# Two diffusion-transformer blocks on one core: value projections laid out channel-major, and the planner's view of a PSUM tile

## The chip, the cores and the metric

One core of a Trainium2 chip runs the whole program: two layers of a block with four kinds of token mixers and an MLP, on 512 image tokens and 256 context tokens. The metric is the device time of one execution in microseconds; three runs of the kernel before took 1811.11, 1812.51 and 1814.94 us.

The engines are TensorE (PE in the views; PEld is its weight load), VectorE (DVE), ScalarE (ACT), GpSimd (POOL) and SyncE (SP), whose queue issues all the transfers of this kernel.

## The reference

Each of the two layers does the following (widths: model 1024, MLP 4096, heads of 64):

```
mod, mod_c = (silu(c), silu(c_ctx)) @ mod_w[l] + mod_b[l]      # six vectors of 1024 each, for image and context
u  = modulate(rmsnorm(h,  norm1), sh1, sc1)  @ w_in            # 512 tokens
uc = modulate(rmsnorm(hc, norm1), csh1, csc1) @ w_in           # 256 context tokens
y_a = ssd_mixer(...)      # conv, silu, two directions of a chunked state scan, gated norm
y_b = diff_mixer(...)     # differential attention: softmax(q1 k1) - lam * softmax(q2 k2), times values
y_c = gqa_mixer(...)      # normed q and k, 4 query heads on 2 key heads
y_d = mla_mixer(...)      # low-rank q and kv, each normed and multiplied by a second weight
h  = h + g1 * (concat(y_a, y_b, y_c, y_d) @ w_out)
h  = h + g2 * (relu(modulate(rmsnorm(h, norm2), sh2, sc2) @ w1) ** 2 @ w2)
```

In the attentions the image queries look at the 256 context and 512 image tokens. The context goes through the same (its queries see the context alone) in layer 0 only. The result is rmsnorm(h) after layer 1.

The columns of w_in that matter here are those of the differential attention (q, k and values, 256 columns each: two groups of 128, dq0, dq1, dk0, dk1, dv0, dv1) and the 128 value columns of the grouped attention.

## The kernel before

**Layout and arithmetic.** Activations lie channel-major: 128 channels in the partitions, 768 tokens (512 image, called XS, then 256 context, called CS) in the columns. A product of full accuracy is three fp32r matmuls: each operand is split into a high and a low part (`split`: ScalarE copies the high part, VectorE or GpSimd subtracts it for the low part), and high x high, high x low and low x high are summed in PSUM. `gemm` does that over the eight tiles of 128 input channels. `big_gemm` sums into a PSUM tile of 1024 columns (tag S, two of them), `side_gemm` into tiles of 512 (tag g, four of them), first the image tokens, then the context. The result of such a projection is channel-major.

**Values.** The product of the attention weights with the values wants the tokens of the values in the partitions. Before, the 384 value columns (differential 256, grouped 128) are therefore computed token-major: `v_start` takes six PSUM regions, one for each 128 tokens, and `v_step` adds one channel tile k to each of them, with the normed activations as the stationary operand and 384 weight columns as the moving one. `v_weights` loads these weights from an array of their own, wv. At the end ScalarE copies 256 columns of each region (dv) and VectorE 128 (gv).

**The start.** x, the modulation weights of layer 0 (four blocks of 2 MB, `mod_dma`) and the first weights are loaded. The norm's statistics are summed (`n_ms`), the modulation is summed block by block (`mod_load`, PSUM tile pm; `mod_done`, PSUM tile pn), and after each block two norm tiles are made (`xn_start`: n_t on VectorE, the high part xn_h on ScalarE, the low part xn_l on VectorE). Between the blocks the values take each norm tile as it comes (`v_step`, PSUM tiles pv, pva, pvb).

**The mixers.** `mixers` runs several tracks as generators: support (all the other projections in the order dk0, dq0, dk1, dq1 and then ORD0, at last `mla_prep`), the attentions one after another (differential j = 0, 1, grouped, MLA), the scan (`ssd_track`), the modulation still to be summed, and the output projection. `Weave` interleaves them by a virtual clock: each step yields a cost, multiplied by its track's weight (TUNE), and the track with the earliest clock goes next. An attention waits until a flag is set: `ready(j)` once the q and k tiles of group j are stacked. Stacking (`stack`) is 16 transfers for each of dk0, dq0, dk1 and dq1. In layer 1 the order is dq0, values, dk0, dq1, dk1, then ORD1, and the weights of the values are split on VectorE.

**The planner.** All instructions go to `Plan.take` first, which notes each one's cost by a formula and what it depends on: two accesses of one tile depend on each other if they overlap and one of them writes. `Plan.order` then plays the program through with these costs. Of an engine's instructions that are ready, the one of the lowest rank goes first (rank is the place in the program; an evacuation of PSUM is put 200 places ahead). Transfers are played at 250 KB per us, one after another, and 1.2 us later for landing. GpSimd's work lengthens VectorE's by 30% of the overlap. Buffers of a tag are given out in the order in which they are first asked for. The order that comes out is each engine's instruction order on the chip; the semaphores follow from the real dependencies.

Weights are staged in float32 in 7 tiles of 128x512 (tag wr) and split into 4 tiles of 2x512 (tag ws).

Of the kernel before, what the change touches and what calls it, by code (L numbers as in the profile page):

```python
# [19 lines left out]
P = 128  # L20
D = 1024
# [16 lines left out]
def _r(c, n=P):  # L38
# [10 lines left out]
    "ckv": _r(C_CKV),  # L49
}  # L50
T_COLS = np.concatenate([_r(C_DV, 256), _r(C_GV)])
# [67 lines left out]
class Later:  # L119


    def __init__(self, pool, shape, dt, name, tag, bufs):
        self.args = (pool, shape, dt, name, tag, bufs)
        self.dt, self.tag, self.bufs = dt, tag, bufs
        self.made = None
# [6 lines left out]
    def ap(self):  # L132
        pool, shape, dt, name, tag, bufs = self.args
        if self.made is None and bufs == 1:
            self.made = pool.tile(list(shape), dt, name=name, tag=tag, bufs=1)
        elif self.made is None:
            self.made = pool.tile(list(shape), dt, name=name, tag=f"{tag}_{self.slot}", bufs=1)
        return self.made
# [12 lines left out]
class Pool:  # L151
    def __init__(self, pool):
        self.pool = pool

    def tile(self, shape, dt, name, tag, bufs):
        t = Later(self.pool, shape, dt, name, tag, bufs)
        return View(t, (), t.base)
# [11 lines left out]
class Plan:  # L169
# [5 lines left out]
    GROUP = 1.0  # L175

    def __init__(self, tc):
        self.tc, self.nc = tc, tc.nc
        self.ops = []
# [5 lines left out]
    def cost(self, eng, name, args, kw, out):  # L185
# [3 lines left out]
        if eng == "PE":  # L189
# [5 lines left out]
            m = w.width()  # L195
# [19 lines left out]
        return 0.45, 1.2  # L215

    def take(self, eng, fn, name, args, kw):
        out = kw["out"] if "out" in kw else args[0]
        writes = [x for x in (out, kw.get("accum_out")) if isinstance(x, View)]
# [3 lines left out]
        if not (eng == "PE" and op is not None and op.eng == "PE" and op.out is out.t and op.cost + cost <= self.GROUP):  # L223
            op = Op(len(self.ops), eng)
            op.out = out.t if isinstance(out, View) else None
            op.bytes = self.bytes if eng == "SP" else 0
# [3 lines left out]
        op.late = late  # L230
        for vs, w in ((reads, False), (writes, True)):
            for v in vs:
# [12 lines left out]
    def order(self):  # L245
        tags = {}
        for op in self.ops:
            op.wait = len(op.before)
            op.rank = op.n - (self.EARLY if op.eng not in ("PE", "SP") and any(t.tag in ("S", "g") for t in op.tiles) else 0)
            for o in op.before:  # L250
                o.after.append(op)
            for t in op.tiles:
                if t.kind is None:
                    t.kind = tags.setdefault(t.tag, Tag(t.tag, t.bufs))
                    t.kind.ask(t)
                t.left += 1
        free = dict.fromkeys(("PE", "DVE", "ACT", "POOL", "SP"), 0.0)
# [4 lines left out]
        def arrive(op):  # L262
            op.at = max((o.end if o.eng == op.eng == "PE" else o.end + o.late + (0.03 if o.eng == op.eng else self.HOP)
# [22 lines left out]
        while len(out) < len(self.ops):  # L286
# [10 lines left out]
            op = min((o for o in ready[e] if o.at <= s), key=lambda o: o.rank)  # L297
# [8 lines left out]
            if e == "SP":  # L306
                dma = max(dma, op.end) + op.bytes / 250e3
# [14 lines left out]
    def issue(self):  # L322
        import os
        out = self.order()
        if os.environ.get("PLAN"):
            report(out)
# [14 lines left out]
class Tag:  # L341
# [6 lines left out]
    def ask(self, t):  # L348
        self.queue.append(t)

    def can(self, t):
        return bool(self.free) and self.queue[self.next] is t
# [21 lines left out]

def report(out):
    free, idle = {}, {}
    for op in out:
        e = op.eng
        w = int(op.start // 50)
        g = op.start - free.get(e, 0.0)  # L380
        idle.setdefault(e, {}).setdefault(w, 0.0)
        idle[e][w] += g
        free[e] = op.start + op.cost
    print("plan ends", max(o.end for o in out), {e: round(sum(o.cost for o in out if o.eng == e), 1) for e in free})
    for e in ("PE", "DVE", "ACT"):
        print(e, [round(idle[e].get(w, 0.0), 1) for w in range(40)])
# [46 lines left out]
def hybrid_block_kernel(ctx: ExitStack, tc: tile.TileContext, a: dict, out: bass.AP, dbg=None):  # L433
# [5 lines left out]
    pp = Pool(ctx.enter_context(tc.tile_pool(name="pp", bufs=1, space=PSUM)))  # L439
# [12 lines left out]
    NSC = 2  # L452
    GAP = 8
# [1384 lines left out]
```

## Time and profile before

| | |
|---|---|
| median of three runs | 1812.51 us (1811.11 to 1814.94) |
| the profiled execution | 1812.9 us, its span 1811.2 us |
| TensorE busy | 1732.4 us, 96% of the span |
| VectorE busy | 1085.0 us, 60% |
| ScalarE busy | 875.6 us, 48% |
| GpSimd busy | 469.4 us, 26% |
| granted TensorE clock, mean | 0.987 |
| moved by DMA | 216.28 MB, 119 GB/s in the mean |

The stages in time: the start to about 69 us, layer 0's mixers to about 456, its output projection and MLP to about 1068, layer 1's mixers to about 1387, its output projection and MLP to the end. The busy times are of one execution. A window row gives, for each engine, the busy time in that stretch and the count of instructions, then the granted clock of TensorE as a share of full speed, the busy share of the DMA engines and GB/s. All helpers are recorded under one line (L331), so the tile names tell the work apart: pv values, pdk and pdq projections, d_, g_ and m_ the three attentions (s scores, t transposes, o output, p probabilities), pe and py the scan, pmv the MLA's values.

### The profile page before, as it was taken

What the parts mean: (1) busy time and instruction counts of PE and PEld (TensorE: products, weight loads), DVE (VectorE), ACT (ScalarE), POOL (GpSimd) and SP (SyncE); (2) the same over time, 40 slices, a digit from 0 to 9 for tenths busy, and PEclk for the clock granted to TensorE, in tenths of its full rate; (3) what the DMA queues carried; (4) which work ended last, traced back from release to release, by engine and by line L of the source; (5) the groups of instructions that cost most, each with busy time, mean ns of one, the idle gap of its engine ahead of it and who ended that gap; (6) DMA issues with size and microseconds to landing.
All of it is one profiled execution on the core that took longest, in us unless ns stands there. A gap on an engine that the chain in (4) does not pass through costs nothing. (4 is left out here: it accounts for less than half of the span.)

```text
span 1811.2 us, 30203 instructions
## 1 busy us (share of the span) xinstructions
PE 1732.4 (96%) x11206; PEld 1464.8 (81%) x11206; DVE 1085.0 (60%) x2112; ACT 875.6 (48%) x1776; POOL 469.4 (26%) x437
## 2 busy tenths in 40 slices
PE   6999999899999999999999999999799999999997
PEld 4878787677878888888888888887678998888886
DVE  4476968787584864543544184887886873333324
ACT  4355767687455223123122353777676762323243
POOL 2322342120244002001002664335110320101056
PEclk9999999999999999999999999999899999999999
DMA  9375431024344543432433334422014552323333
GB/s 354 94 214 150 122 105 37 17 53 162 109 157 141 171 141 96 158 118 87 156 123 99 133 107 133 127 77 59 12 49 152 172 177 93 97 95 94 97 110 126
DMA packets 117330, 216.28 MB, mean 119 GB/s; under 512 B 15424, under 2 KB 24640, under 8 KB 117184
## 3 DMA queue, kind: packets, MB, share of 16 engines
q1 hardware_dynamic: 117184, 214.36, 38.1%
q8 instruction: 88, 1.44, 0.3%
q14 instruction: 58, 0.48, 0.1%
HBM read 185.99 MB, written 8.13 MB: 107 GB/s over the span
## 5 line engine op out<-in xcount | busy, mean ns | idle before, releaser
L331 ACT ACTIVATE w_0s<-w 128x512 fp32r<-128x512 f32 x256 | 160.9, 630 | 387.4 <-PE p L331 352.2
L331 POOL TENSOR_TENSOR r<-r 128x512 f32<-128x512 f32 (+2 forms) x80 | 92.5, 1156 | 652.1 <-ACT a_0h L331 387.4
L331 DVE TENSOR_TENSOR w_0s<-w,w_0s 128x512 fp32r<-128x512 f32 x216 | 149.9, 697 | 184.2 <-ACT w_0s L331 179.1
L331 DVE SCALAR_TENSOR_TENSOR h<-p,modT,h 128x512 f32<-128x512 f32 (+1 forms) x104 | 63.0, 625 | 140.4 <-PE p L331 140.4
L331 ACT ACTIVATE r<-p 128x512 f32<-128x512 f32 (+2 forms) x80 | 47.8, 597 | 166.6 <-PE p L331 165.2
L331 DVE SCALAR_TENSOR_TENSOR junk<-mv,cb 128x512 bf16<-128x512 f32 x128 | 90.2, 716 | 46.2 <-DMA mv<-in_modw_dram 45.4
L331 DVE TENSOR_REDUCE d_m<-d_s 128x1 f32<-128x768 f32 (+1 forms) x80 | 66.4, 846 | 34.8 <-PE d_s L331 33.9
L331 ACT ACTIVATE d_p<-d_s,d_m 128x768 f32<-128x768 f32 (+1 forms) x80 | 65.0, 816 | 37.0 <-DVE d_m L331 28.0
L331 POOL TENSOR_TENSOR w_0s<-w,w_0s 128x512 fp32r<-128x512 f32 x40 | 54.2, 1363 | 28.1 <-ACT w_0s L331 26.3
L331 POOL TENSOR_TENSOR acc<-acc,sq 128x256 f32<-128x256 f32 (+1 forms) x48 | 49.9, 1041 | 42.3 <-ACT sq L331 41.8
L331 PE MATMUL p<-xm_0h,w_0s 128*128 128x512 f32 (+1 forms) x176 | 54.7, 357 | 0.1
L331 PE MATMUL p<-xm_3h,w_0s 128*128 128x512 f32 (+1 forms) x176 | 54.5, 356 | 0.0
L331 PE MATMUL p<-a_0h,w_0s 128*128 128x512 f32 (+1 forms) x176 | 54.1, 354 | 0.3 <-POOL w_0s L331 0.2
L331 PE MATMUL p<-xm_7h,w_0s 128*128 128x512 f32 (+1 forms) x176 | 54.2, 354 | 0.0
L331 PE MATMUL p<-xm_4h,w_0s 128*128 128x512 f32 (+1 forms) x176 | 54.0, 353 | 0.0
L331 PE MATMUL p<-a_5h,w_0s 128*128 128x512 f32 (+1 forms) x176 | 54.0, 353 | 0.0
L331 PE MATMUL p<-a_3h,w_0s 128*128 128x512 f32 (+1 forms) x176 | 54.0, 353 | 0.0
L331 PE MATMUL p<-xm_6h,w_0s 128*128 128x512 f32 (+1 forms) x176 | 53.9, 353 | 0.0
L331 PE MATMUL p<-a_7h,w_0s 128*128 128x512 f32 (+1 forms) x176 | 53.8, 352 | 0.0
L331 PE MATMUL p<-xm_5h,w_0s 128*128 128x512 f32 (+1 forms) x176 | 53.8, 352 | 0.0
L331 PE MATMUL p<-xm_2h,w_0s 128*128 128x512 f32 (+1 forms) x176 | 53.8, 352 | 0.0
L331 PE MATMUL p<-a_4h,w_0s 128*128 128x512 f32 (+1 forms) x176 | 53.8, 352 | 0.0
(2346 smaller groups left out, 5552.6 us busy)
## 6 DMA issues: line engine op xcount, KB each, us to landing
w<-in_w_dram SPq DMA_DIRECT2D x320, 256.0 KB, 2.6
mv<-in_modw_dram SPq DMA_DIRECT2D x96, 256.0 KB, 2.7
mk<-in_modk_dram SPq DMA_DIRECT2D x64, 256.0 KB, 3.4
wr<-in_wout_dram SPq DMA_DIRECT2D x32, 256.0 KB, 2.7
h<-in_xT_dram SPq DMA_DIRECT2D x16, 384.0 KB, 7.6
mw<-in_mod_dram SPq DMA_DIRECT2D x16, 384.0 KB, 6.3
wo<-in_wout_dram SPq DMA_DIRECT2D x32, 192.0 KB, 2.4
wv<-in_wv_dram SPq DMA_DIRECT2D x16, 192.0 KB, 5.0
```

Of the source, the lines that this page charges most:

```text
L331: i = fn(*[x.real() if isinstance(x, View) else x for x in args], **{k: x.real() if isinstance(x, View) else x for k, x in kw.items()}).ins
```

## The change

- Three new projections, dv0, dv1 and gvv, stand among the others and have the same form (channel-major, 128 columns, all 768 tokens). The array wv, `v_weights`, `v_start` and `v_step` go.
- A new `v_prep` makes the token-major values from such a projection: twice three transposes on TensorE into a PSUM tile, and one ScalarE copy of 384 columns. The attentions wait for it: `ready(j)` asks for dv of the group, and `plain_attn` for the flag gv.
- At the start four projections (dk0, dq0, dv0, dk1) are summed as the norm tiles come, in place of the values. They take both S tiles and two g tiles: the image part of each has 512 columns of its own, the context parts share the second half of an S tile two by two, and a matmul with zeros opens each such half (`first_tiles`, `first_step`). Their weights are loaded in two halves of four tiles of 128x512 (`first_load`), the first between the modulation's blocks 0 and 1, and split with GpSimd's subtraction (`first_split`).
- Layer 0's support track begins by copying these four out of PSUM and then goes on with dq1, dv1, gk, ga, gb, gvv, ...; layer 1's order is dq0, dk0, dv0, dq1, dk1, dv1, gk, ga, gb, gvv, ....
- The planner takes two accesses of one PSUM tile by different engines as dependent, whether they overlap or not and also if both read. Transfers are played at 330 KB per us and land 1.4 us later.
- `silu_z` copies its PSUM tile out on ScalarE first and works on the copy.
- 5 tiles of tag wr (7 before), 5 of tag ws (4 before).
- Hooks without effect (BIAS, ASK, empty), NG = 4 for the g tiles as before, and the reports of the planner go.

```diff
@@ Plan.take
+                one = t.space == PSUM
-                for box, o in t.writes if not w else t.writes + t.reads:
-                    if o is not op and box[0] < r1 and r0 < box[1] and box[2] < c1 and c0 < box[3]:
+                for box, o in t.writes if not (w or one) else t.writes + t.reads:
+                    if o is not op and (one and o.eng != op.eng or
+                                        box[0] < r1 and r0 < box[1] and box[2] < c1 and c0 < box[3]):
                         op.before.add(o)
@@ Plan.order, Plan.cost
-                dma = max(dma, op.end) + op.bytes / 250e3
+                dma = max(dma, op.end) + op.bytes / 330e3
...
-        return 0.45, 1.2
+        return 0.45, 1.4
@@ buffers
-    NL, NSM, NP, NWR, NWS, NSD = 43, 4, 6, 7, 4, 3
+    NL, NSM, NP, NWR, NWS, NSD = 43, 4, 6, 5, 5, 3
...
-    ORD0 = "gk ga gb cqx z0 xs0 xs1 cq0 b c z1 ckv".split()
-    ORD1 = "gk ga gb z0 b xs1 cqx xs0 z1 c cq0 ckv".split()
+    ORD0 = "gk ga gb gvv cqx z0 xs0 xs1 cq0 b c z1 ckv".split()
+    ORD1 = "gk ga gb gvv z0 b xs1 cqx xs0 z1 c cq0 ckv".split()
@@ the start
+    FIRST = ("dk0", "dq0", "dv0", "dk1")
+    PAIRS = (("dk0", "dv0"), ("dq0", "dk1"))
...
+    mod_dma(0)
+    first_load(0)
+    mod_dma(1)
+    mod_dma(2)
...
+    def first_tiles():
+        for n, m in PAIRS:
+            ps = ps_s(f"p{n}0")
+            first[n] = [(ps[:, 0:512], XS), (ps[:, 512:768], CS)]
+            first[m] = [(ps_t(f"p{m}0"), XS), (ps[:, 768:1024], CS)]
+            mm(ps[:, 512:1024], ident, sil[:, 0, 2:3].to_broadcast([P, 512]), start=True, stop=False)
+
+    def first_step(k):
+        for n in FIRST:
+            w = fw[n, k // 4]
+            c = slice(P * (k % 4), P * (k % 4) + P)
+            for wi, xi in ((0, 0), (0, 1), (1, 0)):
+                for i, (o, t) in enumerate(first[n]):
...
+                    mm(o, w[:, wi, c], xn[k][xi][:, t], start=begins and i == 0, stop=ends and (i == 0 or bool(both)), parts=both)
...
+    for i in range(4):
+        first_step(2 * i)
+        if i < 3:
+            mod_done(i + 1, m)
+            xn_start(i + 1)
+        first_step(2 * i + 1)
+        if i == 1:
+            first_split(1)
+        if i < 2:
+            m = mod_load(i + 2)
@@ mixers
+        def v_prep(name, n):
+            L.v_[name] = unit(f"t{name}{l}")
+            for i in range(2):
+                ps = ps_t(f"tv{name}{l}_{i}")
+                for t in range(3):
+                    nc.tensor.transpose(ps[:, P * t : P * t + P], raw[name][:, P * (3 * i + t) : P * (3 * i + t) + P], ident)
+                act(L.v_[name][:, 384 * i : 384 * i + 384], ps[:, 0:384], AF.Copy)
+                yield 0.33
...
@@ silu_z
+                z = raw[name][:, s]
                 t = sc(f"zt{name}{l}_{s.start}", s.stop - s.start)
-                ts(t, ps, -80.0, None, op0=ALU.max)
+                act(z, ps, AF.Copy)
+                ts(t, z, -80.0, None, op0=ALU.max)
                 sigmoid_of(t)
-                tt(out=raw[name][:, s], in0=ps, in1=t, op=ALU.mult)
+                tt(out=z, in0=z, in1=t, op=ALU.mult)
@@ support
-                jobs = [dproj("dk0", big_gemm), dproj("dq0", side_gemm), dproj("dk1", side_gemm), dproj("dq1", side_gemm)]
+                for n in FIRST:
+                    for ps, t in first[n]:
+                        dkeep(n)(ps, t)
+                    wv.add(dafter(n)(), K.w_p, K.a_p)
+                yield 0.1
+                jobs = [dproj(n) for n in ("dq1", "dv1")]
             else:
-                jobs = [dproj("dq0", side_gemm)] + v_jobs() + [dproj("dk0", side_gemm), dproj("dq1", side_gemm), dproj("dk1", side_gemm)]
+                jobs = [dproj(n) for n in ("dq0", "dk0", "dv0", "dq1", "dk1", "dv1")]
```

## Rows read from the trace of the kernel before

**Rows 1.** The page: span, busy times, and TensorE's busy tenths in 40 slices.
```profile
span 1811.2 us, 30203 instructions
...
PE 1732.4 (96%) x11206; PEld 1464.8 (81%) x11206; DVE 1085.0 (60%) x2112; ACT 875.6 (48%) x1776; POOL 469.4 (26%) x437
...
PE   6999999899999999999999999999799999999997
```

**Rows 2.** Windows of the start (stretch, length, busy by engine, clock, DMA share, GB/s).
```profile
9.33:25.75 16.42, 12.25 (x72) 6.46 (x73) 8.30 (x13) 8.89 (x16) 2.41 (x2) 0.98 1.04 383
25.75:69.15 43.40, 39.86 (x281) 34.13 (x281) 20.33 (x40) 15.18 (x30) 10.82 (x9) 0.89 0.63 221
```

**Rows 3.** Windows of the mixers, layer 0 and then layer 1.
```profile
103.00:270.00 167.00, 161.18 (x1286) 130.64 (x1285) 128.62 (x263) 109.93 (x249) 53.38 (x55) 0.98 0.51 143
270.00:380.00 110.00, 98.17 (x814) 78.80 (x813) 89.28 (x221) 79.52 (x181) 23.87 (x27) 0.97 0.14 39
1110.00:1250.00 140.00, 138.41 (x869) 113.78 (x869) 110.28 (x197) 96.03 (x199) 62.27 (x56) 1.00 0.38 100
1250.00:1330.00 80.00, 68.80 (x524) 54.45 (x523) 65.13 (x156) 58.53 (x130) 17.61 (x22) 0.91 0.12 34
1280.00:1290.00 10.00, 6.29 (x17) 3.77 (x18) 7.46 (x24) 4.70 (x9) 0.00 (x0) 0.72 0.07 26
```

**Rows 4.** TensorE's waits in 1040 to 1420 (total us, times, longest).
```profile
PE cqn_ms L331 <- ACT cqn_s L331: 4.4, 2, 2.3
...
PE pmv L331 <- DVE ee L331: 1.7, 1, 1.7
```

**Rows 5.** TensorE's timeline at the start (start, duration, instructions, idle before).
```profile
25.75 1.01 PE L331 MATMUL pv<-wv_0s,xn_0h 128*128 128x384 f32 x2 [2.11 <-ACT xn_0h L331]
...
54.51 1.93 PE L331 MATMUL pm<-mw,sil 128*32 128x256 f32 x32
...
60.21 0.62 PE L331 MATMUL pv<-wv_3s,xn_6h 128*128 128x384 f32 x2 [0.98 <-ACT xn_6h L331]
...
66.02 0.51 PE L331 MATMUL pv<-wv_3s,xn_7h 128*128 128x384 f32 x2
...
69.15 0.51 PE L331 MATMUL pdk<-xn_0h,wdk00s 128*128 128x512 f32 x2
...
77.52 0.39 PE L331 MATMUL pdq<-xn_0h,wdq00s 128*128 128x512 f32 x1
```

**Rows 6.** Timelines of VectorE and GpSimd near 21 to 27.
```profile
21.30 2.58 DVE L331 SCALAR_TENSOR_TENSOR n_r<-n_q,n_r 128x512 f32<-128x512 f32 x2
...
26.31 1.14 DVE L331 SCALAR_TENSOR_TENSOR xn_0l<-n_t,modT,xn_0h 128x512 fp32r<-128x512 f32 x2
...
21.19 2.41 POOL L331 TENSOR_TENSOR wv_0s<-wv,wv_0s 128x384 fp32r<-128x384 f32 x2 [17.02 <-ACT wv_0s L331]
```

**Rows 7.** TensorE's timeline at 1043: float32 matmuls of a norm (512 and 256 columns).
```profile
1043.45 1.02 PE L331 MATMUL n_ms<-acc,ones 128*128 128x512 f32 x2
```

**Rows 8.** The chain that ended last, at 1342: six transposes.
```profile
1342.33 0.66 PE m_t L331 x6
```

**Rows 9.** Timelines of SP's queue and TensorE at the first scores.
```profile
98.45 0.59 SPq L331 DMA_DIRECT2D sdq<-hldq_0l  x1
...
102.73 0.59 PE L331 MATMUL d_s<-sdk,sdq 128*128 128x512 f32 x2 [2.32 <-DMA sdq<-hldq_0l]
```

**Rows 10.** Scores of layer 1's attentions (ns min/median/max, first and last start).
```profile
L331 PE MATMUL d_s<-sdk,sdq x64: 274/336/798, 1134.3 to 1225.1; 128*128 128x512 f32 x32, 128*128 128x256 f32 x32
...
L331 PE MATMUL g_s<-gks,gqs x64: 276/394/775, 1253.9 to 1316.5; 128*128 128x512 f32 x32, 128*128 128x256 f32 x32
...
L331 PE MATMUL m_s<-mk_0h,mq_0h x8: 278/380/497, 1327.8 to 1350.7; 96*128 96x512 f32 x4, 96*128 96x256 f32 x4
```

**Rows 11.** VectorE's waits in 103 to 456.
```profile
DVE ee L331 <- ACT ea L331: 4.7, 8, 0.9
```

**Rows 12.** The waits of SP's queue in 456 to 1050.
```profile
SPq L331 <- DVE w_0s L331: 235.0, 95, 4.6
```

More of the change, by code (lines that the diff above doesn't have):

```diff
@@ L1 @@
 import math
+import re
 from contextlib import ExitStack
@@ L133, in ap @@
         pool, shape, dt, name, tag, bufs = self.args
-        if self.made is None and bufs == 1:
-            self.made = pool.tile(list(shape), dt, name=name, tag=tag, bufs=1)
-        elif self.made is None:
+        if self.made is None:
             self.made = pool.tile(list(shape), dt, name=name, tag=f"{tag}_{self.slot}", bufs=1)
@@ L248, in order @@
             op.wait = len(op.before)
-            op.rank = op.n - (self.EARLY if op.eng not in ("PE", "SP") and any(t.tag in ("S", "g") for t in op.tiles) else 0)
+            op.rank = op.n + self.BIAS.get(op.kind, 0)
+            if op.eng not in ("PE", "SP") and any(t.space == PSUM for t in op.tiles):
+                op.rank -= self.EARLY
             for o in op.before:
@@ L254, in order @@
                     t.kind = tags.setdefault(t.tag, Tag(t.tag, t.bufs))
-                    t.kind.ask(t)
+                    t.kind.ask(t, op.n + self.ASK.get((op.kind[0], re.sub(r"\d", "", t.args[3])), 0))
                 t.left += 1
+        for tag in tags.values():
+            tag.queue.sort(key=lambda x: x[0])
         free = dict.fromkeys(("PE", "DVE", "ACT", "POOL", "SP"), 0.0)
@@ L346, in __init__, with ask @@
         self.free, self.queue, self.next = [(0.0, i, None) for i in range(bufs)], [], 0
-    def ask(self, t):
-        self.queue.append(t)
+    def ask(self, t, rank):
+        self.queue.append((rank, t))
     def can(self, t):
-        return bool(self.free) and self.queue[self.next] is t
+        return bool(self.free) and self.queue[self.next][1] is t
     def take(self, t):
@@ L372, in __getattr__ @@
         return lambda *args, **kw: self.plan.take(self.eng, fn, name, args, kw)
[L375 to L386, printed above, removed]
 class Weave:
@@ L738, in big_gemm @@
         ps = ps_s(name)
-        b = toks[0].start
-        yield from gemm([(ps[0:m, t.start - b : t.stop - b], t) for t in toks], w, xs)
-        evac(ps[0:m, 0 : toks[-1].stop - b], slice(b, toks[-1].stop))
+        b, e = toks[0].start, toks[-1].stop
+        yield from gemm([(ps[0:m, c : min(c + 512, e - b)], slice(b + c, min(b + c + 512, e))) for c in range(0, e - b, 512)], w, xs)
+        evac(ps[0:m, 0 : e - b], slice(b, e))
     def side_gemm(name, w, xs, toks, evac, m=P):
@@ L836, in sigmoid_of, with first_load, first_split @@
         act(t, t, AF.Exp, scale=-1.0)
-    def v_weights(l, q):
-        return weights(f"wv{l}_{q}", a["wv"][l, :, q], 384, gtt if l == 0 else tt)
-    wv = [v_weights(0, q) for q in range(4)]
-    for i in range(3):
-        mod_dma(i)
-        next(wv[i])
+    FIRST = ("dk0", "dq0", "dv0", "dk1")
+    PAIRS = (("dk0", "dv0"), ("dq0", "dk1"))
+    fw = {}
+    def first_load(i):
+        for n in FIRST:
+            fw[n, i] = sb.tile([P, 512], F32, name=f"w{n}0_{i}", tag="wr", bufs=NWR)
+            ld(fw[n, i], a["win"][0, :, T_OFF[n] + 512 * i : T_OFF[n] + 512 * i + 512])
+    def first_split(i):
+        for n in FIRST:
+            x = sb.tile([P, 2, 512], F32R, name=f"w{n}0s{i}", tag="ws", bufs=NWS)
+            split(x[:, 0], x[:, 1], fw[n, i], gtt)
+            fw[n, i] = x
+    mod_dma(0)
+    first_load(0)
+    mod_dma(1)
+    mod_dma(2)
     psq = [ps_t(f"n1_0_ms{i}")[:, 0 : s.stop - s.start] for i, s in enumerate((XS, CS))]
@@ L891, in value_of @@
-    def value_of(gen):
-        while True:
-            try:
-                next(gen)
-            except StopIteration as e:
-                return e.value
-    for i, s in enumerate((XS, CS)):
-        run(rstd_of(f"n1_0_q{i}", psq[i], rb, s))
-    ws = [value_of(wv[0])]
-    mod_done(0, mod_load(0))
+    first = {}
+    def first_tiles():
[4 more added lines that the diff above has]
+            mm(ps[:, 512:1024], ident, sil[:, 0, 2:3].to_broadcast([P, 512]), start=True, stop=False)
@@ L1155, in plain_attn @@
         def plain_attn(name, j, jobs, vcols, kout, flag, s_cost):
-            while flag not in done:
+            while flag not in done or "gv" not in done:
                 yield None
```

129 lines of the change are left out of this document (58 added, 71 removed).

## The prediction

> **What bounds the kernel now.** I read the engine totals first. TensorE is busy 1732.4 us of 1811.2 [rows 1], so the time can only move where TensorE idles, where its granted clock is below 1, or where its work changes. The idle time is 78.8 us. The stage windows say where it is: 13.5 us before the first values product at 25.75 (12.25 busy by then), 3.5 while the values are summed [rows 2]; in layer 0's mixers 6 us in 103 to 270 and 12 in 270 to 380; in layer 1's mixers 11 in 1250 to 1330, where the clock is 0.91 [rows 3]. The MLPs' slices are at 9 throughout [rows 1]. So three places matter: the start, and the second half of each mixer, in which VectorE is busy for 65.1 of 80 us and what TensorE waits for are chains of small steps (MLA's query norm, 4.4 us) [rows 3, 4].
>
> The profiled execution took 1812.9 us, 1.7 beyond its span. That is 0.4 above the median of the runs (1812.5). I sum against the span and carry the difference to the median.
>
> **The start.** Before, six token tiles sum values as norm tiles come: a step (one norm tile) lasts 3.13 us on TensorE (66.02 to 69.15) [rows 5]. After, a step has four projections of 768 columns. The columns of such a projection are those of dk0, 8.37 us for eight steps (69.15 to 77.52) [rows 5], so a step is 4 x 8.37 / 8 = 4.19 us. The work done by the end is the same as before's values (three projections' worth of columns: 8 x 3.13 = 25.0 = 3 x 8.37) plus dk0. So I compare with 77.52.
>
> Before, the 43.40 us from 25.75 to 69.15 hold 25.0 us of values, 3.5 idle, and a granted clock of 0.89, that is 0.11 x 43.4 = 4.8 lost [rows 2]. The remaining 10.1 is the modulation's matmuls. The idle time is waits of about 0.75 us in which a step of 3.13 was too short to cover the chain from the modulation (pn) to the norm tile; the last, 0.98 for xn_6, comes after the modulation's last block, which the planner placed late, at 54.51 [rows 5]. After, steps are 1.05 us longer and cover that. The planner's transfer rate goes from 250 to 330 KB per us, the row shows 383 [rows 2], so it will place those blocks earlier. I leave 0.4 idle, and a clock loss of 3.4, since the second slow stretch follows the waits that go. Sum: 33.5 + 10.1 + 0.4 + 3.4 = 47.4, the end at 73.2.
>
> Two things are added. The weight splits on GpSimd for the first half come as four of 128x512 in a row instead of two of 384. VectorE's n_r pair took 2.58 us beside GpSimd's subtractions where the alike pair xn_0l took 1.14 [rows 6], a factor of 2.3. Two subtractions of 384 columns took 2.41, so four of 512 take 2.41 x 2 x 512 / 384 = 6.4 us, from 21.2 on [rows 6]. If all of it lies beside VectorE, that gets 6.4 / 2.3 = 2.8 us done in it and loses 3.6, of which 1.4 (2.58 - 1.14) was lost before too. So 0 to 2.2 more; I take 1.5 us on the first norm tile. The two zeroing matmuls are float32 of 512 columns; a norm's 768 columns took 1.02 [rows 7], so 0.7 each, 1.4 together. They lie in the 2.11 us in which TensorE waits for xn_0 [rows 5]; I take 0.5, ends 0 and 2.8 (if the half clock holds there). The end is then 75.2 against 77.52: **2.4 us gained**; ends 5.5 gained and 2 lost.
>
> DMA: four tiles of 256 KB stand ahead of modulation block 1 where two of 192 KB did, 0.66 MB or 1.7 us at 383 [rows 2]. Ends 0 and 1.7 lost; I take 0, since the first step's products lie between that block's landing and the norm tiles made from it.
>
> **Transposes.** Values channel-major cost the same columns in the projection, and then 3 tiles x 6 x 2 layers = 36 transposes on TensorE. Six in a row take 0.66 us on the chain [rows 8], 0.11 each: **4.0 us added**, 2 in each layer. Ends: 0 if they all fall into idle time, 8 if as much again is lost in waits for the raw tiles and for the copies. The evacuations change from 6 ScalarE and 6 VectorE copies to 12 ScalarE copies a layer, and silu_z gets one more each time, 6 in all, which lets its PSUM tile go sooner; ScalarE is busy 58.5 of 80 us in the tightest stretch, less than VectorE [rows 3]: no cost, ends 2 either way.
>
> **Attention in layer 0 starts earlier.** dk0, dq0, dv0 and dk1 are all there at 75, where before they came one after another from 77.5 on. What follows is the chain to the stacked tiles and 16 small transfers for each of dk0 and dq0, 0.6 us of issue each on SP's queue [rows 9]: some 7 + 10 + 6 us, so the first scores come at about 98, not 102.7. By then TensorE has done the same projections as before, so this is the start's gain seen again, and not a second one. What may go is the first scores' wait of 2.32 on that transfer [rows 9] and others like it: I take **1.5 us gained**, ends 4 and 0.
>
> **Layer 1.** The order dq0, values, dk0 becomes dq0, dk0, dv0. Without the 25 us of values ahead, dk0 is done 25 us earlier, so the scores, first at 1134.3 [rows 10], begin at about 1109, with dv1, gk and the grouped values still to do beside them. TensorE's work does not change. What changes is that the attention's VectorE work is spread over more of the projections: 110 us of VectorE in the 140 before 1250, 65 in the 80 after [rows 3]. Idle time of 12.8 us in 1110 to 1330 (1.6 + 11.2) and 7 lost in the clock at 0.91 (0.09 x 80) are there to be had. I take a quarter, **5 us gained**; ends 15 gained and 12 lost (the second nearly the first rival).
>
> **The planner's PSUM rule.** VectorE's ee waits for ScalarE's ea, 4.7 us in layer 0, though the two only read the same PSUM tile [rows 11]: real and unplanned. TensorE waits 1.7 for ee at layer 1's pmv [rows 4]. With it counted, the planner puts other work there: **1.5 us gained**, ends 4.7 gained and 1 lost.
>
> **Buffers.** Weight staging falls from 7 tiles to 5, split weights rise from 4 to 5. In layer 0's MLP SP's queue already waits 235 us for weight tiles to come free [rows 12] while TensorE idles next to nothing, so a lead of 5 tiles is less but still a lead. I take 0; up to 6 lost if TensorE waits in the MLPs or at the tail.
>
> Sum: -2.4 + 4.0 - 1.5 - 5.0 - 1.5 = -6.4. Span 1804.8, that execution 1806.5, the median **1806**.
>
> **Rivals.** *1. Layer 1's support track falls behind (slower).* The attention runs 25 us ahead of the projections, so the grouped attention (g_s from 1253.9 to 1316.5) is over that much sooner against the MLA chain, which ends with m_s at 1328 [rows 10], and only the scan fills TensorE. The stretch 1250 to 1330 has 0.86 x 0.91 = 0.78 of full-clock work; its worst ten us have 0.63 x 0.72 = 0.45 [rows 3]. 25 x (0.78 - 0.45) = 8.3 us lost in place of 5 gained: 1806 + 13 = 1819. It decides from the point where m_s comes over 20 us after the last g_s (11 before). For: the weights of the tracks stay as they were. Against: VectorE has less left by then. 0.20.
>
> *2. Transposes eat the start.* The order in the mixers comes out different and no better, or the third block is planned late again, so that the change doesn't fill the waits: -2.4 - 1.5 + 4 = 0, 1812.5. For: most waits are chains [rows 4] that an order cannot shorten. 0.18.
>
> *3. GpSimd holds up VectorE at the start.* The second four splits fall beside the norm chains of xn_4 to xn_7 as well, each losing up to 3.6; the start loses 1.5 instead of gaining 2.4: 1810. For: the 2.58 [rows 6]. Against: there they wait for buffers, one by one. 0.08. The Trainium skill (GPSIMD Engine Reference, "1. Specifications") says that GpSimd and VectorE share SBUF interfaces and contend when the VectorE instruction has two SBUF inputs; n_r has, and the trace agrees with 2.58 against 1.14.
>
> *4. The spread pays fully*: 18 of layer 1's 20 us go instead of 5; 1793. 0.06.
>
> **Numbers.** The forecast has 0.48, 1800 to 1811. About 0.2% (3.6 us) is what a measurement of this kernel can tell from no change. Faster: 0.39 of the forecast, 0.04 of rival 2, 0.03 of 3, 0.06 of 4, 0.52. Slower: 0.16 of rival 1, 0.05 of 2, 0.02 of the others, 0.23. Same 0.25. The range 1790 to 1822 takes in all five, without rival 1's and 4's outer parts, the bounds of layer 1 and those of the buffers.
>
> **What would show it.** Right: dq1's first matmul at 74 to 77; waits for xn tiles under 1 us in all; layer 1's first scores 20 to 30 us sooner after its first projection; less idle between the last g_s and m_s. Wrong: idle over 15 us in layer 1's MLA chain (rival 1); TensorE waiting for weights in an MLP (buffers); first norm tile after 28 (rival 3); layer 1's idle unchanged with only the 4 us of transposes to see (rival 2).

## The result: 0.8% slower

The changed kernel takes 1827.4 us (median of 4 runs, 1826.8 to 1828.9), the kernel before, measured beside it, 1813.7; the ratio is 1.0078, 95% interval 1.0062 to 1.0094. The forecast was 1806 us with a range of 1790 to 1822: the sign was wrong, and the time lies outside the range. The profiled execution took 1828.9 us, its span is 1827.0; before, 1811.2 [rows 1].

The page of after, where [rows 1] stood before (span; TensorE's busy time; its busy tenths and clock tenths in 40 slices of 45.7 us):

```profile
span 1827.0 us, 30275 instructions
...
PE 1740.1 (95%) x11246; PEld 1461.0 (80%) x11246; DVE 1102.4 (60%) x2092; ACT 884.7 (48%) x1791; POOL 473.6 (26%) x441
...
PE   7979999799999999999999989999799999999997
...
PEclk9989999999999999999999999999899999999999
```

TensorE is busy 7.7 us more and idle 8.1 us more (86.9 against 78.8). Against [rows 1] the tenths dip in the third slice (91 to 137, 7 for 9) and by one at 320 and at 1051; the 7 late in layer 1's mixers (1279 to 1325) was there before. Marks on TensorE (the starts of first and last products, in us) split the 15.8 us of span:

| stage | before | after | difference |
|---|---|---|---|
| four projections of the start done | 77.5 | 73.6 | -4.0 |
| layer 0's last m_o | 455.6 | 468.5 | +12.9 |
| from there to layer 1's first pdq | 612.3 | 610.9 | -1.4 |
| from there to layer 1's last m_o | 319.2 | 325.4 | +6.2 |
| from there to the end | 424.1 | 422.2 | -1.9 |

So the start gained more than forecast, layer 0 then lost 16.9 us (394.9 from the start's mark to the last m_o, 378.1 before), and layer 1 lost 6.2. The marks are of one execution each. In the traces of the experiments on after below, the start's mark lies between 71.7 and 74.2, so below layer 0 is compared by its length from that mark and not by its end.

**The start.** TensorE's timeline of after (start, duration, instructions, idle before), to be held against [rows 5]:

```profile
1.80 2.07 PE L338 MATMUL pdk<-sil,ident 128*128 128x512 f32 x2 [1.80 <-POOL ident masks.py:199]
3.67 1.91 PE L338 MATMUL pdq<-sil,ident 128*128 128x512 f32 x2
...
26.67 0.80 PE L338 MATMUL pdv<-xn_0h,wdv00s 128*128 128x512 f32 x1 [4.35 <-ACT xn_0h L338]
...
73.57 0.39 PE L338 MATMUL pdq<-xn_0h,wdq10s 128*128 128x512 f32 x1
```

The zeroing matmuls run at 1.80 to 5.6, ahead of everything. The first product on a norm tile comes 0.9 us later than before, dq1's first at 73.57.

**Layer 0 after the start.** Windows of after and then of before, from the start's end on (stretch, length, busy time of each engine, TensorE's clock, DMA share, GB/s); the first two rows of after answer to [rows 2]:

```profile
9.33:26.67 17.34, 11.05 (x56) 5.68 (x55) 9.53 (x11) 9.69 (x17) 5.80 (x4) 0.95 1.04 395
26.67:73.60 46.93, 46.15 (x313) 35.90 (x314) 23.14 (x39) 14.68 (x28) 9.76 (x8) 0.95 0.47 165
74.00:100.00 26.00, 21.29 (x145) 17.90 (x144) 17.27 (x20) 11.21 (x24) 15.97 (x10) 0.94 0.49 120
100.00:130.00 30.00, 22.29 (x126) 16.88 (x126) 18.67 (x36) 14.45 (x31) 0.00 (x0) 0.77 0.72 177
130.00:175.00 45.00, 43.38 (x336) 33.96 (x335) 28.20 (x51) 25.79 (x55) 12.07 (x9) 1.00 0.52 157
...
96.70:103.50 6.80, 5.19 (x15) 4.35 (x16) 1.30 (x2) 1.37 (x3) 0.00 (x0) 0.50 0.65 153
113.70:124.00 10.30, 6.08 (x47) 3.81 (x46) 5.18 (x11) 1.75 (x6) 0.00 (x0) 0.50 0.83 216
```

```profile
74.00:100.00 26.00, 26.00 (x169) 21.96 (x168) 13.34 (x16) 8.52 (x15) 13.26 (x9) 1.00 0.51 136
100.00:130.00 30.00, 25.70 (x193) 19.47 (x192) 22.39 (x42) 16.15 (x36) 4.48 (x3) 0.89 0.80 219
130.00:175.00 45.00, 45.00 (x361) 36.93 (x361) 30.77 (x62) 28.84 (x68) 9.35 (x8) 1.00 0.54 148
...
103.50:106.90 3.40, 3.36 (x9) 1.87 (x7) 2.46 (x5) 2.18 (x5) 0.00 (x0) 0.50 0.63 154
110.30:113.70 3.40, 3.09 (x13) 2.70 (x13) 3.40 (x7) 0.97 (x3) 1.96 (x1) 0.50 0.76 183
```

In these 101 us TensorE idles 14.0 us after (4.7, 7.7 and 1.6) and 4.3 before. The last two rows of each block are the stretches at half clock. TensorE is busy there for 5.19 + 6.08 = 11.3 us after and for 6.5 before, and half of that is lost: 5.6 and 3.2. Together that is 12.1 us more. With the forecast's 2.0 us for layer 0's transposes it makes 14 of the 16.9. From 175 to the last m_o the two idle about alike (18.1 and 19.0). The rest lies in TensorE's busy time: 1.1 of it are 32 modulation matmuls that before ran ahead of the start's mark, and for some 2 us no cause is shown. What TensorE waited for there (total us, times, longest; mk are the modulation's weights, pk its sums):

```profile
PE d_s L338 <- DMA sdq<-hldq_0l: 4.7, 1, 4.7
PE pk L338 <- DMA mk<-in_modk_dram: 4.1, 2, 3.8
PE d_s L338 <- ACT d_p L338: 3.5, 3, 2.3
```

Two of the three name transfers. SP's queue in that stretch of after (start, time of issue, transfer; sdk and sdq are the stacked tiles, filled from hldk_0 and hldq_0 for the first group, from hldk_1 and hldq_1 for the second):

```profile
94.03 0.53 SPq L338 DMA_DIRECT2D sdq<-hldq_0h  x1
...
103.50 0.59 SPq L338 DMA_DIRECT2D sdq<-hldq_0l  x1
104.20 1.17 SPq L338 DMA_DIRECT2D sdk<-hldk_1h  x2
...
113.04 1.23 SPq L338 DMA_DIRECT2D sdk<-hldk_1l  x2
114.37 1.97 SPq L338 DMA_DIRECT2D mk<-in_modk_dram  x4
116.43 0.51 SPq L338 DMA_DIRECT2D sdq<-hldq_1h  x1
...
126.74 0.60 SPq L338 DMA_DIRECT2D sdq<-hldq_1l  x1
127.44 1.98 SPq L338 DMA_DIRECT2D mk<-in_modk_dram  x4
129.51 0.38 SPq L338 DMA_DIRECT2D wgb<-in_win_dram  x1
```

The queue is solid from 83 to 129. All four stacks, 64 transfers of 0.6 us, stand in it one after another, with only one group of mk between them; dk1's 16 hold that group up until 114.37, and TensorE's pk waits for it until 117.6. Projection work that needs no transfer still to come (the second half of pgk) stands behind pk in TensorE's order. The kernel before sends the same 64 transfers, but spread over 83 to 141, and lets weights out between them. Its queue:

```profile
94.55 1.97 SPq L331 DMA_DIRECT2D mk<-in_modk_dram  x4
...
106.85 0.53 SPq L331 DMA_DIRECT2D wgb<-in_win_dram  x1
107.48 0.39 SPq L331 DMA_DIRECT2D wcqx<-in_win_dram  x1
...
117.49 1.01 SPq L331 DMA_DIRECT2D mk<-in_modk_dram  x2
```

**Layer 1.** The scores of after, against [rows 10]: d_s start 23 us sooner after the first projection, and g_s come at the same distance from it as before (184.2 us; before 186.0).

```profile
L338 PE MATMUL d_s<-sdk,sdq x64: 274/337/503, 1122.8 to 1215.9; 128*128 128x512 f32 x32, 128*128 128x256 f32 x32
...
L338 PE MATMUL g_s<-gks,gqs x64: 276/336/502, 1263.6 to 1334.0; 128*128 128x512 f32 x32, 128*128 128x256 f32 x32
...
L338 PE MATMUL m_s<-mk_0h,mq_0h x8: 279/337/669, 1345.7 to 1364.9; 96*128 96x512 f32 x4, 96*128 96x256 f32 x4
```

The layer as a whole, before and then after (the columns of the windows above): TensorE idles 18.5 us before and 23.7 after, 5.2 of the 6.2 us.

```profile
1067.90:1387.10 319.20, 300.73 (x2106) 248.89 (x2104) 241.41 (x480) 214.41 (x462) 96.83 (x91) 0.98 0.29 82
```

```profile
1079.40:1404.80 325.40, 301.72 (x2124) 247.38 (x2122) 253.16 (x469) 221.02 (x470) 105.81 (x97) 0.97 0.29 80
```

The waits of after in 1030 to 1420, against [rows 4]: two single long ones, in both of which transposes of the grouped attention stand at the head of TensorE's order.

```profile
PE g_t L338 <- DVE g_m L338: 6.9, 1, 6.9
PE g_t L338 <- ACT cqn_s L338: 6.1, 1, 6.1
```

### The profile page after: what moved, and what is told of

It reads as the page before. It is cut to its first block, busy times and chain, and to the rows that moved or that the text cites. A ratio compares the mean times of both kernels' runs of the same rounds, so it can differ in the third digit from the quotient of the medians.

```text
span 1827.0 us, 30275 instructions
## 1 busy us (share of the span) xinstructions
PE 1740.1 (95%) x11246; PEld 1461.0 (80%) x11246; DVE 1102.4 (60%) x2092; ACT 884.7 (48%) x1791; POOL 473.6 (26%) x441
## 5 line engine op out<-in xcount | busy, mean ns | idle before, releaser
L338 POOL TENSOR_TENSOR r<-r 128x512 f32<-128x512 f32 (+2 forms) x80 | 88.8, 1110 | 647.3 <-ACT a_0h L338 391.8
L338 PE MATMUL g_t<-ident,g_p 128*128 128x128 f32 x208 | 34.8, 299 | 21.2 <-DVE g_p L338 6.9
L338 PE MATMUL p<-xm_1h,w_0s 128*128 128x512 f32 (+1 forms) x176 | 54.2, 354 | 0.0
L338 PE MATMUL p<-a_6h,w_0s 128*128 128x512 f32 (+1 forms) x176 | 53.9, 353 | 0.0
L338 PE MATMUL p<-a_1h,w_0s 128*128 128x512 f32 (+1 forms) x176 | 53.9, 352 | 0.0
```

What stands on the lines that cost most here:

```text
L338: i = fn(*[x.real() if isinstance(x, View) else x for x in args], **{k: x.real() if isinstance(x, View) else x for k, x in kw.items()}).ins
```

## The experiments

The theory after the comparison: the change sends layer 0's four stacks through SP's queue together, ahead of weights (16.9 us), and in layer 1 the early scores take cover away from the grouped and the latent attention. Rivals: the planner's PSUM rule, the buffers, the transposes, crowded VectorE, and an order so sensitive that any edit moves it. All ratios are to the kernel before, measured beside each run, with 95% intervals; 0.001 is 1.8 us. What a run gives back is the difference of two such ratios. The changed kernel itself stands at 1.0078.

**b_rule, on the kernel before:** the PSUM rule alone.

```
+ one = t.space == PSUM
- if o is not op and <boxes overlap>:
+ if o is not op and (one and o.eng != op.eng or <boxes overlap>):
```

> The kernel before with one edit: the planner counts a PSUM tile as one engine's at a time. Queue theory (the loss comes from 64 small stack transfers that stand back to back on SP's queue in the changed kernel): this part has no hand in it, 1811 to 1816 us, ratio 0.999 to 1.001; the forecast gave this part -1.5 us. Rival (the planner's rule reorders the mixers for the worse): 1820 or more, ratio 1.004 or more. Rival (the order is so sensitive that any small change of the planner moves the time by several us): anywhere from 1806 to 1822.

Measured 1812.1 us, 0.9986 (0.9977 to 0.9994). On the kernel before the rule costs nothing: alone it gains 2.5 us (1.1 to 4.2; forecast 1.5). Its layer 1 takes 315.9 us for 319.2. The waits that the forecast named are gone there: VectorE's ee waits 0.4 us for ea where it waited 4.7 [rows 11], and TensorE's pmv no longer waits for ee.

**a_spcost, on after:** `return 0.45, 1.4` -> `return 0.62, 1.4` for a transfer.

> The changed kernel; the planner's price of one transfer's issue on SP goes from 0.45 to 0.62 us, about what the traces show for the stacks (0.59). Nothing else. Queue theory: TensorE's order then puts filler ahead of the first scores and of the modulation's matmuls, which are late: their two waits (4.7 and 3.8 us) fall under 2 us each, the time to 1815 to 1822 us. Rival (the lost time has to do with the work itself, the transposes and the projections' new order): 1825 to 1830. Rival (sensitivity): no relation between the waits and the time.

Measured 1827.7 us, 1.0074 (1.0062 to 1.0086). The two waits fell (4.7 to 3.0 in three pieces, 4.1 to 2.2), but scores waiting for d_p rose from 3.5 to 6.9: the price alone turns one wait into another. A miss.

**a_latedk1, on after:** dk1's rotation and stacking are chained behind dq1's projection.

```
- wv.add(dafter(n)(), K.w_p, K.a_p)
+ if n != "dk1": wv.add(dafter(n)(), K.w_p, K.a_p)
...
+ proj("dq1", QT, dkeep("dq1"), side_gemm, lambda: both("dk1", "dq1"))
```

> The changed kernel, but in layer 0 the rotation, split and stacking of dk1 come only after dq1's projection, so that its 16 transfers no longer stand ahead of the modulation's weights. Queue theory: the modulation's weights land some 10 us sooner, the 3.8 us wait of TensorE for them goes, the scores' wait of 4.7 stays: 1820 to 1825 us. Rival (the loss lies in the attention's chain itself, since three stacks' worth of work at once crowds VectorE and ScalarE): the same, as VectorE's work is taken out of the stretch 76 to 90 too, but the second half of the stacks would then be late: 1827 to 1832. Rival (sensitivity): anything.

Measured 1822.6 us, 1.0049 (1.0038 to 1.0060): some 5 us back; layer 0 takes 389.4 us for 394.9.

**a_half, on after:** two transfers of 64 rows for each stacked tile of layer 0, instead of four of 32.

```
- for b, s in enumerate(pat): ld(d[32 * b : 32 * b + 32], hl[s][32 * r : 32 * r + 32])
+ for b in range(2): ld(d[64 * b : 64 * b + 64], hl[b][64 * (r // 2) : 64 * (r // 2) + 64])
```

> The changed kernel, but in layer 0 each stacked tile is filled by two transfers of 64 rows instead of four of 32: the same bytes, 32 issues fewer on SP's queue. The stacked tiles then hold other rows than the reference wants. Queue theory: 32 x 0.6 = 19 us of the queue go, the loss of layer 0 with them: 1811 to 1817 us. Rival (bytes, not issues, hold the transfers up): 1825 to 1830. Rival (the planner's rule or the work itself): 1825 to 1830.

Measured 1818.5 us, 1.0024 (1.0015 to 1.0034): 10 us back with the same bytes; layer 0 takes 385.5 us for 394.9. The number of issues is what costs, not the bytes. The time is just above what was expected: a 64-row issue takes 0.46 to 0.94 us (two took 1.2 and 1.8), so the 32 issues hold the queue for 23.4 us where the 64 held it for 38.4, and less than half of the queue's time went.

**b_half, on the kernel before:** the same edit.

> The kernel before, but in layer 0 each stacked tile is filled by two transfers of 64 rows instead of four of 32, so that the tiles hold other rows. In the changed kernel this gave back 9 us. Theory (the changed kernel pays for its stacks because all of them come before the weights): before gains 0 to 3 us, 1810 to 1814. Rival (any kernel with these stacks pays 9 us for them): 1803 to 1806.

Measured 1813.3 us, 0.9990 (0.9980 to 1.0000). Halving the same issues gives the kernel before 1.8 us (0 to 3.6), the changed kernel 10: the price comes from where they stand.

**a_l1old, on after:** layer 1's first jobs in the order of before.

```
- ("dq0", "dk0", "dv0", "dq1", "dk1", "dv1"), then gk ga gb gvv ...
+ ("dq0", "dv0", "dv1", "gvv", "dk0", "dq1", "dk1"), then gk ga gb ...
```

> The changed kernel, layer 1's first jobs in the order of before: dq0, then the value projections dv0, dv1 and gvv, then dk0, dq1, dk1. Layer 0 is untouched. Theory (the scores that start 25 us sooner in layer 1 displace the overlap of the grouped and the latent attention with projections): the layer's 325.4 us from its first dq0 product to its last m_o product fall to 317 to 321, the time to 1819 to 1823 us. Rival (the transposes, the copies and the channel-major values cost it, whatever the order): 325 again, 1826 to 1829 us. Forecast's view (sooner scores help): 1830 or more.

Measured 1822.0 us, 1.0045 (1.0031 to 1.0060): 6 us back; layer 1 takes 320.4 us for 325.4. The traces of all the runs agree. The eleven of the changed kernel and its variants with the new order in layer 1 take 322.4 to 326.8 us for it, and each has the two long waits of g_t (6.1 and 6.9 us, in a_hop21 6.1 and 5.2). The three with the old order (this one, a_comb1, a_comb3) take 318.9 to 321.4 and have neither.

**a_actq, on after:** the 32 transfers of the second pair's stacks go out from ScalarE's queue (`nc.scalar.dma_start` where j = 1). The planner counts 0.1 us of ScalarE for each such issue.

> The changed kernel, but layer 0's 32 transfers that fill the second pair's stacked tiles (dk1 and dq1) are issued from ScalarE's queue instead of SP's. Queue theory: 32 x 0.6 = 19 us leave SP's queue, the modulation's weights come at about 105 instead of 114, their wait of 3.8 goes: 1817 to 1823 us. Rival (the bytes or the transfers' own time hold it up, not the queue that issues them): 1826 to 1830. Rival (ScalarE is what the first attention waits for, and it pays for the issues now): 1828 to 1835, with longer waits of scores for d_p.

Measured 1829.8 us, 1.0086 (1.0072 to 1.0100). The third outcome, in another place than expected. ScalarE's timeline (ACTq: its queue's issues):

```profile
85.68 0.38 ACT L340 ACTIVATE dq<-pdq 128x256 f32<-128x256 f32 x1
85.96 4.21 ACTq L340 DMA_DIRECT2D sdk<-hldk_1h  x5
90.26 5.13 ACTq L340 DMA_DIRECT2D sdk<-hldk_1l  x6
95.44 1.24 ACTq L340 DMA_DIRECT2D sdk<-hldk_1h  x2
97.12 1.42 ACTq L340 DMA_DIRECT2D sdk<-hldk_1l  x2
98.58 0.63 ACT L340 ACTIVATE wga0s<-wga 128x512 fp32r<-128x512 f32 x1 [12.52 <-DMA sdk<-hldk_1h]
...
101.26 0.60 ACT L340 ACTIVATE dv<-pdv 128x512 f32<-128x512 f32 x1 [1.31 <-DMA sdk<-hldk_1l]
```

ScalarE copies nothing for 12.5 us, in which 15 transfers are issued; the planner had counted 1.5 us for them. TensorE's value transposes wait 9.3 and 10.4 us for dv. The run says nothing for or against SP's queue. The Trainium skill (Perfetto Trace Analysis, "DMA Optimizations") says that spreading transfers over the engines that can issue them may help where descriptor generation is the bottleneck. Here it did not help: the engine chosen had copies in the same queue, and the plan had not reckoned with the time of the issues. A run with a true price there was not made.

**a_bufs74, on after:** 7 staged and 4 split weight tiles, as before the change.

> The changed kernel with the numbers of weight tiles of before, 7 staged and 4 split, instead of 5 and 5. Forecast: no cost, so 1825 to 1830 us. Rival (five staged tiles are too short a lead, in the mixers or in the MLPs): 1819 to 1824, most of it back in the stage where weights come late. Queue theory: no change beyond 2 us, as the weights stand behind stacks either way.

Measured 1832.7 us, 1.0104 (1.0089 to 1.0119): with the old numbers it is 4.7 us slower. Most of it shows from layer 1's last m_o to the end (425.4 for 422.2). That points to a gain from 5 and 5, but does not show one: the two intervals touch, and the next run moves the time by 3 us without any reason.

**a_hop21, on after:** HOP 0.20 -> 0.21.

> The changed kernel; the planner's price of a hop between engines goes from 0.20 to 0.21 us. It stands for a change without meaning. Theory (the loss has causes that belong to the change): 1825 to 1830 us, ratio to the kernel before still 1.006 to 1.009. Rival (the order is so sensitive that any small change moves the time by several us, and the changed kernel drew a bad one): off by 4 us or more to either side, most likely down, 1815 to 1823.

Measured 1825.3 us, 1.0062 (1.0048 to 1.0075). A change without meaning moves it by about 3 us, in the trace most of it in layer 1 (322.4 us for 325.4), but not out of the loss. Differences of 3 us between two orders are left unexplained below.

**a_mkfirst, on after:** BIAS = {(1, "SP", "mk_"): -400}.

> The changed kernel; in layer 0's mixers the transfers of the modulation's weights (mk) are ranked ahead of the stacks on SP's queue, so that they go as soon as a buffer of theirs is free. Theory (late mk stops TensorE twice over: its own wait of 3.8 us, and the projections whose PSUM tiles are handed out after pk's): that wait goes, the first scores come up to 4 us later since six pairs of mk now stand among the stacks: 1820 to 1825 us. Rival (the attention's own chain of scores, maxima and exponentials is what is short of cover, mk has no share): 1826 to 1830.

Measured 1826.9 us, 1.0070 (1.0057 to 1.0083). TensorE's waits in 74 to 175:

```profile
PE pgb L338 <- DVE gkn_q L338: 6.1, 1, 6.1
PE d_s L338 <- DMA sdq<-hldq_0l: 5.7, 3, 4.9
```

pk waits no more, but pgb now stands behind the grouped keys' norm for 6.1 us. Moving one transfer past the others in the full queue only changed who waits. A miss.

**a_comb1, on after:** a_latedk1, a_mkfirst and a_l1old together.

> The changed kernel with three edits at once: dk1's rotation and stacking after dq1's projection, mk ranked ahead of the stacks, layer 1's first jobs in the order of before. If they are causes of their own, their savings add up (5.0, 5.4 and 0 to 4 us): 1813 to 1818 us. Rival (they cure the same thing, or each order is a fresh draw): 1819 to 1824.

Measured 1813.8 us, 0.9999 (0.9989 to 1.0008). The savings add up: two causes in two places. Layer 0 takes 387.3 us (389.4 in a_latedk1), layer 1 321.4 (320.4 in a_l1old).

**a_notr, on after:** no transposes and no copies of the values; the attention reads the channel-major tiles.

> The changed kernel without the transposes of the values and their 12 copies: the attention reads the channel-major tiles as they are, so its output is another one. Forecast: the transposes cost 4.0 us (ends 0 and 8): 1822 to 1825 us. Rival (waiting for raw values and for the copies is a large part of the loss): 1819 or less. Rival (they fall into idle time): 1826 to 1829.

Measured 1827.1 us, 1.0067 (1.0053 to 1.0080): 2 us, of the size of a_hop21's. The transposes are no large cause; between 0 and 4 us it can't tell.

**a_last300, on after:** only the rank of the second pair's stacks on SP's queue.

```
+ BIAS = {(1, "SP", "sdkx___"): 300, (1, "SP", "sdqx___"): 300}   # names of tiles with j = 1
```

> The changed kernel; on SP's queue alone, layer 0's stacks of the second pair (dk1, dq1) are ranked behind the modulation's and the projections' weights. The other engines' instructions stay as they are. Queue theory (the second pair's 32 transfers, some 20 us of the queue, stand ahead of weights that TensorE needs sooner): mk and the weights come some 10 to 20 us sooner, 1818 to 1823 us. Rival (VectorE and GpSimd are crowded by dk1's rotation and split): no gain, 1826 to 1830. Rival (the first attention's own chain is what binds, whatever comes on the queue): 1826 to 1830, with longer waits of scores for d_p.

Measured 1823.9 us, 1.0040 (1.0025 to 1.0055): 7 us back from ranks on SP's queue alone (the planner moves a few of TensorE's instructions with them). Its windows show where the rest went:

```profile
100.00:130.00 30.00, 29.51 (x234) 23.64 (x233) 25.59 (x45) 20.98 (x47) 4.32 (x4) 0.98 0.76 219
130.00:175.00 45.00, 39.50 (x273) 30.42 (x275) 26.52 (x47) 20.52 (x46) 11.45 (x8) 0.89 0.50 142
```

The hole at 100 to 130 is closed; a smaller one opens behind it, where pk waits 5.3 us for mk. VectorE has the same work as in after, so its crowding is not what cost these 7 us.

**a_lastspc, on after:** this rank and the price of 0.62 us.

> The changed kernel with the second pair's stacks ranked last on SP's queue and 0.62 us as the price of an issue; layer 1's order as in the changed kernel. Theory (queue order and price work only together: the price makes the planner put TensorE's filler where the queue really is, the rank gets the weights there): layer 0 ends at 453 to 456 us as in the run with the order too, the time is that run's 1809 plus the 5.4 of the order, 1813 to 1816 us. Rival (the savings are separate, 3.6 and 0): 1822 to 1825.

Measured 1815.3 us, 1.0010 (1.0001 to 1.0019): 12 us back, where the two alone gave 7 and 1. Layer 0 takes 381.3 us for 394.9; before it took 378.1.

**a_comb3, on after:** rank, price and layer 1's old order.

> The changed kernel with the second pair's stacks ranked last on SP's queue, layer 1's first jobs in the order of before, and 0.62 us as the price of an issue. If the savings add up (5 to 8 for the queue, 5.4 for the order, 0 to 2 for the price): 1812 to 1818 us. Rival: not under 1820.

Measured 1809.0 us, 0.9958 (0.9944 to 0.9973). The windows from the start's end on, against those of after above:

```profile
74.00:100.00 26.00, 24.32 (x158) 19.45 (x156) 16.34 (x17) 11.11 (x22) 14.40 (x10) 1.00 0.47 115
100.00:130.00 30.00, 26.74 (x213) 21.15 (x213) 24.10 (x44) 19.64 (x42) 5.17 (x4) 0.89 0.79 228
130.00:175.00 45.00, 43.47 (x357) 34.54 (x355) 32.12 (x61) 26.29 (x60) 13.93 (x10) 1.00 0.64 178
```

Idle is 6.5 us for 14.0, the half clock's loss 2.5 for 5.6 (101.5 to 108.3, TensorE busy for 5.0). Layer 0 takes 381.5 us for 394.9, 3.4 more than before, of which 2.0 are the forecast's transposes. In layer 1, from the first g_s to the last m_o, after and then this kernel:

```profile
1263.60:1404.80 141.20, 124.88 (x1046) 102.26 (x1044) 106.92 (x234) 101.32 (x226) 23.99 (x28) 0.93 0.18 53
```

```profile
1252.60:1382.60 130.00, 119.06 (x998) 93.59 (x998) 105.17 (x233) 99.48 (x222) 23.62 (x28) 0.96 0.19 58
```

With the scores early, this stretch has 16.3 us of idle time, and 13.2 us of work at half clock, which cost 6.6; with the values first, 10.9, and 8.8 at half clock, which cost 4.4. That is 7.6 of the 11.2 us by which it is longer. What comes ahead of it in the layer is 4.7 us shorter with the scores early (184.2 for 188.9), so that the layer loses 6.5 in all.

**b_best, on the kernel before:** the PSUM rule and the prices 0.62 and 1.4; **b_best55:** the same with buffers 5 and 5.

> The kernel before with the planner's PSUM rule, and with its prices of a transfer at 0.62 us of issue and 1.4 of latency. The rule alone measured 2.5 us faster than before; if the true price of an issue helps the order, 1807 to 1811 us; if not, 1811 to 1814, as the rule alone. Rival (a higher price only shifts the order about): anything within 4 us of 1812.

> The kernel before with the PSUM rule, the price of 0.62 and 1.4 us for a transfer, and the buffers of the changed kernel (5 staged weight tiles, 5 split). The first two measured 0.9972. If 5 and 5 helps here as it did in the changed kernel (5 us), 1803 to 1807 us; forecast's view (no effect): 1808 to 1812; rival (5 staged tiles are too short a lead when the order is another): 1812 or more.

Measured 1809.8 us, 0.9972 (0.9961 to 0.9983), and 1808.0 us, 0.9953 (0.9938 to 0.9968). The rule and the buffers of the change, with a truer price, make the kernel before 0.5% faster without the new values. What each of the three gives is not told apart: the intervals of the two runs overlap.

**mix, on after:** a_comb3 with layer 1's values token-major as before.

> As the run with rank, price and layer 1's old order, but in layer 1 the values are token-major as in the kernel before, summed in six tiles, with no transposes there; layer 0 keeps the channel-major values and the four first projections. Theory (layer 1 pays 2 us for transposes and 1 to 2 for longer chains, and the planner's PSUM rule saves 3 there): layer 1's 318.9 us fall to 315 to 317, the time to 1804 to 1808 us. Rival (channel-major values cost layer 1 nothing): 1808 to 1811.

Measured 1805.9 us, 0.9963 (0.9950 to 0.9975). Layer 1 takes 313.4 us for 318.9, more of a gain than the theory has. With the PSUM rule, the four kernels with token-major values in layer 1 (b_rule, b_best, b_best55, mix) take 313.4 to 316.9 for it, the three with channel-major values in the old order 318.9 to 321.4, so that layer 1 itself pays for them. But the intervals of mix, a_comb3 and b_best55 overlap, and the rest of mix's profile is 4.5 us longer. Whether channel-major values in layer 1 cost the whole kernel anything stays open. All three beat both kernels.

## Why the prediction was wrong

**The start: right, a little small.** Forecast 2.4 us gained, measured 4.0 in the profiled execution; by the marks of 71.7 to 74.2 in the variants' traces it would be 3.3 to 5.8. The first norm tile came 0.9 us late for 1.5 forecast, beside 6.2 us of GpSimd's splits (6.4 forecast); idle after it was 0.8 for 0.4, the clock's loss 0.05 x 46.9 = 2.3 for 3.4. The zeroing took 3.8 us for 1.4, but ahead of everything, so it cost nothing. dq1's first product at 73.6 is just outside the 74 to 77 named.

**Attention in layer 0 starts earlier: the step that failed.** I had the first scores at 98 (98.3) and forecast 1.5 us gained; 14.9 were lost (the 16.9 less 2.0 for transposes). I counted dk0's and dq0's 32 transfers up to the first scores and stopped there. dv0 and dk1 are done at the same moment, so dk1's 16 follow at once, dq1's 16 after them, and the queue holds mk and the next weights up for 20 us: 32 more issues than the sum had, at the 0.59 us that stood in [rows 9]. The sentence that by then TensorE has done the same projections was nearly true (6.1 of them for 6.4), and no bound: it says nothing about what the next work waits for. a_half (10 us), b_half (2) and a_last300 (7) show that it is the stacks' issues, and where they stand, that cost; a_lastspc brings 13.6 of the 16.9 back with rank and price. No rival of mine had this mechanism; the range had no term for it.

**Layer 1: the wrong sign.** Forecast 5 us gained by earlier scores (ends 15 gained, 12 lost). The scores came 23 us sooner, as forecast, and the layer took 6.2 more. Undoing the order gave 6 us alone, and 9 on top of rank and price (0.9958 against 1.0010). I read the idle time of [rows 3] as there for VectorE's spread to fill; but the grouped attention did not move with the first one (184.2 us after the first projection, 186.0 before), and less was left to cover the waits after it. That the cover is what is missing is my reading; that the order makes the two waits is shown (a_l1old). Rival 1 had the sign and the stretch, but its condition fails: m_s comes 11.7 us after the last g_s (11.3 before); the loss lies in the grouped attention's own transposes (6.9 and 6.1).

**Transposes:** 4.0 forecast; a_notr gives 2, within the ends of 0 and 8; it tells neither 0 nor 4 apart. **The PSUM rule:** 1.5 forecast, 2.5 measured on the kernel before, by the waits that were named. **Buffers:** forecast 0, with up to 6 lost. Two runs point the other way, by 4.7 and 3.4 us (a_bufs74, b_best55), each with intervals that touch or overlap; my ends left no room for a gain. Which of the two numbers would do it was not run.

**Rivals 2 to 4** did not come. Rival 3's contention was there: n_r's pair took 2.10 us beside GpSimd's splits, and beside the later ones xn_4l's pair took 3.20 and xn_5l's 2.16, against 1.14 for xn_6l's without. But the longer steps covered it: TensorE idled 0.8 us in the whole stretch.

## What to carry to other kernels

When results that came one after another are made ready together, count everything that follows from each of them on the in-order queue that they share, up to the next thing that the bound engine needs, and not only up to the first consumer. A small wait taken away in a full queue can come back as another one: here the price or one transfer moved ahead gave 1 us each, the rank 7, and rank and price together 12. Starting a stage earlier did not help here, where the stage behind it could not start earlier too.

## What the runs showed of the hardware

A 32-row transfer of 96 KB holds SP's queue for 0.51 to 0.60 us (median 0.59; two of after's 64 took longer), a 64-row one of a_half for 0.46 to 0.94 (median 0.64; two took longer). On ScalarE's queue in a_actq the issue of a 32-row one took as long (median 0.57), but they followed each other at 0.84 us in bunches (4.21 for 5, 5.13 for 6), and no activation began from 86.0 to 98.5. In after, TensorE's clock fell to its half level during the wait of 4.7 us ahead of the first scores (96.7 to 103.5) and between waits of 2.3 and 3.8 us (113.7 to 124.0); the 11.3 us of work in these stretches cost 5.6 us, on top of the idle time.
